# Start addresses of the moving operands, 64 bytes further from a multiple of 128, in a two-block transformer kernel

## The chip, the core and the metric

The kernel runs on one core of a Trainium2 chip. The metric is the time of one execution on the device in microseconds (us), the median of several runs.

## What is computed

Two transformer blocks follow each other on one sequence of 256 positions and width 2048, all in float32. Cut to the products with weights, which are nearly all of the work:

```python
# first block
h = rmsnorm(x, g_mix);   z = h @ w_in                  # 2048 -> 3584
kv = rmsnorm(mem, g_mem) @ w_kv                        # 2048 -> 1024, 256 memory rows
mix = concat(gated conv of z, pooled z @ pool_w, cross attention(q, k, v))
x = x + mix @ w_out                                    # 2048 -> 2048
u = causal_dwconv(rmsnorm(x, g_ffn) @ w_up) + bias     # 2048 -> 2 x 5632
x = rmsnorm(x + (silu(gate) * val) @ w_down, g_final)  # 5632 -> 2048
# second block
proj = rmsnorm(x, norm_attn_2) @ w_in_2                # 2048 -> 6144
x = x + concat(dilated attention, differential attention) @ w_out_2
h = rmsnorm(x, norm_ffn_2)
x = x + (silu(h @ w_gate_2) * (h @ w_up_2)) @ w_down_2
return rmsnorm(x, norm_final_2)
```

## The kernel before

**Split operands.** The products run in the type fp32r. To keep precision, every weight and every activation is split into a high part (its fp32r rounding) and a low part (the rest), and three of the four part products are added. An activation tile holds both parts side by side: 256 columns of high parts, then 256 of low parts, so 512 columns of 4 bytes.

**Blocks.** The weights come as blocks of 128 x 128. Each block makes two TensorE products into one accumulator of 512 columns: a *long* one (line 206: the block's high part, stationary, against all 512 columns, moving) and a *short* one (line 209: its low part against the 256 high columns). `products` takes blocks four at a time and orders them so that, in a steady stream of 16 blocks per output tile, TensorE does 8 longs, 8 shorts, 8 longs, and so on. Each product has its own load of 128 stationary columns (PEld), which the engine runs beside the product before it. So TensorE reads two streams from SBUF at a time: the moving columns of one product and the stationary columns of the next.

**Streams of weights.** A unit is 16 blocks, 1 MB. `prefetch` loads it three units ahead into a `raw` buffer by SyncE's queue, ScalarE copies it into a `hi` buffer (line 173), VectorE subtracts to get `lo` (line 185), half a unit at a time and two units ahead. The order of all engines is written out by hand, by a loop over quarters of a unit (`emit_all`); nothing in the change touches it.

**Moving tiles.** `A` holds the normalised activations that feed `w_in`, `w_up`, the q and k products of the second block, and `w_gate_2`/`w_up_2`: 3776 blocks. `M` holds the memory's (64 blocks). One buffer with the tag `mix` holds, one after another, `M`, `mix` (256 blocks of `w_out`), `hid` (1408 blocks of the two down products, in parts of 16, 14 and 14 rows of the hidden layer) and `y` (256 blocks of `w_out_2`). Six tiles `poolHL` feed 14 blocks. `hid` in the stages of 16 rows, `mix` and `A` meet the same order of instructions: 16 blocks per output tile.

**V products.** For the V projections the roles change (`vs_unit`, lines 273 to 275): 128 columns of `A` or `M` are stationary and 512 columns of `hi` or `lo` move: three products each, 384 products on `A` and 96 on `M`.

**Where tiles lie.** Every tile is a range of bytes in each partition, and the pools lie one behind the other. `raw`, `hi` and `lo` have sizes that are multiples of 128, so all of them start 32 bytes behind a multiple of 128. `X` and `A` follow and start at 32 too. Then comes the tag `stg` (first tile `mem`, 16448 bytes, which is 64 more than a multiple of 128), so the tag `mix` and all behind it start at 96. Columns are taken in steps of 512 bytes, so these remainders hold for every operand.

Of the kernel before, what the change touches and what calls it, by code (L numbers as in the profile page):

```python
# [10 lines left out]
F32 = mybir.dt.float32  # L11
F32R = mybir.dt.float32r
# [6 lines left out]
P = 128  # L19
D = 2048  # L20
S = 256
KT = D // P
# [77 lines left out]
def tile_two_blocks(ctx: ExitStack, tc: tile.TileContext, a: dict, out: bass.AP):  # L100
# [6 lines left out]
    big = pool("big", 1)  # L107
# [10 lines left out]
    vec = cst.tile([P, NCOL], F32, name="vec")  # L118
    ones = cst.tile([P, P], F32, name="ones")
    ident = kc[:, K_IDENT:K_IDENT + P]  # L120
    X = big.tile([P, KT, S], F32, name="X")
    A = big.tile([P, KT, 2 * S], F32R, name="A")

    def gain(name, kt):
        c = GAINS.index(name) * KT + kt
        return vec[:, c:c + 1]
# [61 lines left out]
    def weights(i, c0, c1):  # L188
        j = 2 * i + c0 // HB
        hi, lo = halves[j]  # L190
        c = slice(c0 % HB, (c1 - 1) % HB + 1)
        return hi[:, c], lo[:, c]
# [7 lines left out]
    def products(blocks):  # L200


        mm = nc.tensor.matmul

        def long(acc, hi, lo, x, first, last):
            mm(acc, lhsT=hi, rhs=x, start=first, stop=last)  # L206

        def short(acc, hi, lo, x, first, last):
            mm(acc[:, S:], lhsT=lo, rhs=x[:, :S], start=False, stop=False)  # L209

        opening = [b for b in blocks if b[4]]
        closing = [b for b in blocks if b[5]]
        between = [b for b in blocks if not b[4] and not b[5]]
        if longs[0] and not closing:
            for b in opening + between:
                long(*b)
            for b in blocks:
                short(*b)
            longs[0] = False
        else:  # L220
            for b in opening:
                long(*b)
            if opening and not closing:
                for b in between:
                    long(*b)
            for b in blocks:
                short(*b)
            if not opening or closing:
                for b in between:
                    long(*b)  # L230
            for b in closing:
                long(*b)
            longs[0] = bool(closing) or not opening
# [27 lines left out]
    def vs_unit(src, act, g, accs):  # L261

        def emit(i, b):
            if g == 0 and b == 0:
                for _ in range(2):
                    ac = acc_p.tile([P, 512], F32, tag="acc", name="acc")
                    accs.append(ac)
            kt = 4 * g + b
            x = act()[:, kt, :]
            hi, lo = weights(i, b * 512, (b + 1) * 512)  # L270
            for t in range(2):
                xh, xl = x[:, t * P:(t + 1) * P], x[:, S + t * P:S + (t + 1) * P]
                nc.tensor.matmul(accs[t], lhsT=xh, rhs=hi, start=kt == 0, stop=False)  # L273
                nc.tensor.matmul(accs[t], lhsT=xh, rhs=lo, start=False, stop=False)  # L274
                nc.tensor.matmul(accs[t], lhsT=xl, rhs=hi, start=False, stop=kt == KT - 1)  # L275

        return add_unit(src, UB * P, emit)
# [111 lines left out]
    def put_act(kt, g, x, a, norm):  # L389

        hi = a[:, kt, :S]
        nc.scalar.activation(hi, x, AF.Copy, scale=g)  # L392
        norm.add(x)
        yield
        nc.vector.scalar_tensor_tensor(out=a[:, kt, S:], in0=x, scalar=g, in1=hi.bitcast(F32),  # L395
                                       op0=ALU.mult, op1=ALU.subtract)
# [36 lines left out]
    def softmax(src, scale, normalise=True):  # L433

        mx = sm.tile([P, 2], F32, tag="mx", name="mx")
        nc.vector.tensor_reduce(out=mx, in_=src, op=ALU.max, axis=AX.X, negate=True)
        if scale != 1.0:
# [34 lines left out]
        return pt  # L472


    stg = big.tile([P, KT + KT * S], F32, tag="stg", name="mem")
    gm = stg[:, :KT]
    mem_t = stg[:, KT:].rearrange("p (k t) -> p k t", k=KT)
    M = big.tile([P, KT, 2 * S], F32R, tag="mix", name="M")
    lam_in = t2.tile([P, 4, 64], F32, tag="t2", name="lam_in")

    def load_mem(k0, k1):
# [32 lines left out]
    def x_load(q):  # L514
        nc.sync.dma_start(X[:, 4 * q:4 * q + 4, :], a["x"][:, 4 * q:4 * q + 4, :])

# [7 lines left out]
    def lambdas():  # L524
# [3 lines left out]
        sl = sm.tile([P, 2], F32, tag="lam_s", name="lam_s", bufs=1)  # L528
        nc.vector.tensor_reduce(out=sl, in_=pr, op=ALU.add, axis=AX.X)
        nc.scalar.activation(sl, sl, AF.Exp)  # L530
# [10 lines left out]
    def mem_act(kt):  # L541
        x, g, hi = mem_t[:, kt, :], gm[:, kt:kt + 1], M[:, kt, :S]
        nc.vector.tensor_scalar(out=hi, in0=x, scalar1=g, scalar2=None, op0=ALU.mult)
        nc.vector.scalar_tensor_tensor(out=M[:, kt, S:], in0=x, scalar=g, in1=hi.bitcast(F32),
                                       op0=ALU.mult, op1=ALU.subtract)
# [4 lines left out]
    def x_act(kt):  # L550
        return put_act(kt, gain("g_mix", kt), X[:, kt, :], A, n_x)

# [26 lines left out]
    for g in range(4):  # L579
        vs_unit(a["w_v"][g], lambda: M, g, v_accs)  # L580

        def emit(i, b, g=g):
            kt = 4 * g + b
            if kt == 0:
# [3 lines left out]
                for _ in range(2):  # L588
                    ac = s_p.tile([P, 2 * S], F32, tag="s", name="acc_s")
                    k_accs.append(ac)  # L590
            products([(k_accs[m], *weights(i, (4 * b + m) * P, (4 * b + m + 1) * P), M[:, kt, :],
                       kt == 0, kt == KT - 1) for m in range(4)])
# [15 lines left out]
    mix = {}  # L608
# [129 lines left out]
    def residual(gname, norm, scaled_to=None):  # L738
        def add(dst, m, acc):
            nc.vector.tensor_tensor(out=dst, in0=acc[:, :S], in1=X[:, m, :], op=ALU.add)  # L740
            nc.vector.tensor_tensor(out=dst, in0=acc[:, S:], in1=dst, op=ALU.add)  # L741

        def twice(m, acc):
            x = t1.tile([P, S], F32, tag="t", name="xr")
            add(x, m, acc)
            nc.vector.tensor_scalar(out=X[:, m, :], in0=x, scalar1=gain("g_final", m), scalar2=None, op0=ALU.mult)
            norm.inner.add(x)
# [381 lines left out]
```

## Time and profile before

| | us |
|---|---|
| median of 3 runs (2203.36 to 2205.53) | 2204.1 |
| the profiled execution | 2204.54 |
| its span in the trace | 2202.7 |
| TensorE busy with products | 2182.8 |
| VectorE busy | 1603.5 |
| ScalarE busy | 1143.2 |

The profiled execution is 0.4 us above the median, and its span leaves 1.8 us outside the trace. The page of the profile gives busy times, the granted clock of TensorE in 40 slices, the chain of work that ended last, and groups of equal instructions. The timeline gives instructions in order of time, equal neighbours merged into one row with their count; the start of one row less the start of the row before is the time that the earlier run took from the engine. The durations in a row overlap, since a product begins before the one ahead of it has ended, so all paces here are taken from starts.

### The profile page before, as it was taken

The page shows a single profiled execution, that of the slowest core. Times are in us where ns is not written, and L with a number is a line of the kernel's source. Part 1 is how long each engine was busy: PE and PEld are TensorE (multiplying, and loading weights), DVE is VectorE, ACT ScalarE, POOL GpSimd, SP SyncE. Part 2 cuts the span into 40 slices and gives each one's busy share as a digit, 9 for nine tenths or more (in the row PEclk, how much of TensorE's full clock was granted, in tenths as well). Part 3 has the DMA queues.
Part 4 walks back from the last instruction along what each step waited for, and adds up shares of the span by engine and source line. Part 5 has one row for each costly group of instructions (what it writes and reads, how often), then busy time and mean ns, then how long its engine had stood idle before and what let it go on. Part 6 is the DMA issues. An engine that isn't in the chain of part 4 may idle for free.

```text
span 2202.7 us, 31334 instructions
## 1 busy us (share of the span) xinstructions
PE 2182.8 (99%) x12426; PEld 1909.5 (87%) x12426; DVE 1603.5 (73%) x2553; ACT 1143.2 (52%) x1738; POOL 106.7 (5%) x114
## 2 busy tenths in 40 slices
PE   8999999999999999999999999999999999999997
PEld 7888888888888888888888888888888888888886
DVE  8877778886588757878779677786665666666666
ACT  6555556564465536565456655464443444344442
POOL 4000010000000000003100000010000000000012
PEclk9999999999999999999999999999999999999998
DMA  7545555555555555555544444555555555555553
GB/s 285 197 169 177 191 188 193 189 192 191 191 191 186 190 182 192 188 192 188 194 167 158 161 165 153 179 203 186 185 186 192 191 189 191 191 192 186 185 184 115
DMA packets 60195, 408.99 MB, mean 186 GB/s; under 512 B 6672, under 2 KB 8592, under 8 KB 11792
## 3 DMA queue, kind: packets, MB, share of 16 engines
q1 hardware_dynamic: 60048, 406.99, 53.9%
q8 instruction: 97, 1.59, 0.3%
q14 instruction: 50, 0.41, 0.0%
HBM read 404.86 MB, written 2.10 MB: 185 GB/s over the span
## 4 chain that ended last, share of the span: by engine, by line
PE 97%; DVE 1%; DMA 1%; issue 0%; SPq 0%; ACT 0%; DVEq 0%; ACTq 0%
PE acc L206 60%; PE acc L209 31%; PE acc L273 1%; PE acc L274 1%; PE acc L275 1%; PE s_ps L430 1%; DVE lo L185 0%; DMA X<-in_x 0%; PE pT_ps L466 0%; PE o_ps L920 0%; PE o_ps L878 0%; DMA raw<-in_w_k 0%; DVE end L998 0%; PE nps L342 0%; PE o_ps L638 0%
## 5 line engine op out<-in xcount | busy, mean ns | idle before, releaser
L173 ACT ACTIVATE hi<-raw 128x1024 fp32r<-128x1024 f32 x758 | 799.2, 1057 | 583.2 <-PE acc L206 413.9
L185 DVE TENSOR_TENSOR lo<-raw,hi 128x1024 fp32r<-128x1024 f32 x758 | 933.5, 1239 | 145.4 <-ACT hi L173 133.4
L206 PE MATMUL acc<-A,hi 128*128 128x512 f32 x3776 | 961.6, 394 | 0.0
L206 PEld LDWEIGHTS acc<-A,hi 128*128 128x128 f32 x3776 | 677.3, 189 | 119.8 <-issue 1.0
L209 PEld LDWEIGHTS acc<-A,lo 128*128 128x128 f32 x3776 | 518.5, 190 | 39.2 <-issue 0.7
L209 PE MATMUL acc<-A,lo 128*128 128x256 f32 x3776 | 535.0, 283 | 0.0
L206 PE MATMUL acc<-hid,hi 128*128 128x512 f32 x1408 | 360.2, 392 | 0.0
L206 PEld LDWEIGHTS acc<-hid,hi 128*128 128x128 f32 x1408 | 250.6, 188 | 41.5
L414 ACT ACTIVATE z<-acc 128x256 f32<-128x256 f32 x244 | 91.8, 382 | 274.2 <-PE acc L206 274.1
L209 PEld LDWEIGHTS acc<-hid,lo 128*128 128x128 f32 x1408 | 195.3, 188 | 17.2
L209 PE MATMUL acc<-hid,lo 128*128 128x256 f32 x1408 | 199.6, 279 | 0.0
L740 DVE TENSOR_TENSOR X<-acc,X 128x256 f32<-128x256 f32 x128 | 54.0, 422 | 177.4 <-PE acc L206 177.3
L416 DVE TENSOR_TENSOR z<-acc,z 128x256 f32<-128x256 f32 x244 | 103.0, 422 | 103.4 <-ACT z L414 102.6
L715 DVE SCALAR_TENSOR_TENSOR c<-z,vec,c 128x255 f32<-128x255 f32 (+1 forms) x188 | 90.0, 480 | 5.1 <-ACT c L710 1.2
L404 DVE TENSOR_TENSOR hid<-hid 128x256 fp32r<-128x256 f32 x88 | 37.4, 425 | 77.1 <-ACT hid L402 77.1
L422 DVE TENSOR_TENSOR z<-z,R_ffn 128x256 f32<-128x256 f32 x176 | 74.7, 424 | 6.0
L206 PE MATMUL acc<-y,hi 128*128 128x512 f32 x256 | 65.4, 394 | 0.0
L206 PE MATMUL acc<-mix,hi 128*128 128x512 f32 x256 | 64.2, 392 | 0.0
L317 POOL TENSOR_TENSOR sq_attn<-sq_attn,sqt 128x256 f32<-128x256 f32 x30 | 29.4, 993 | 707.9 <-ACT sqt L315 707.7
L392 ACT ACTIVATE A<-X,vec 128x256 fp32r<-128x256 f32 x64 | 32.4, 507 | 57.8 <-DVE X L741 57.3
L741 DVE TENSOR_TENSOR X<-acc,X 128x256 f32<-128x256 f32 x128 | 54.3, 424 | 4.4
L395 DVE SCALAR_TENSOR_TENSOR A<-X,vec,A 128x256 fp32r<-128x256 f32 x64 | 50.6, 802 | 8.3 <-ACT A L392 8.3
(174 smaller groups left out, 1347.5 us busy)
## 6 DMA issues: line engine op xcount, KB each, us to landing
raw<-in_w_up SPq DMA_DIRECT2D x88, 1024.0 KB, 4.9
raw<-in_w_down SPq DMA_DIRECT2D x88, 1024.0 KB, 4.9
raw<-in_w_gu SPq DMA_DIRECT2D x88, 1024.0 KB, 4.9
raw<-in_w_out SPq DMA_DIRECT2D x32, 1024.0 KB, 4.9
raw<-in_w_in SPq DMA_DIRECT2D x22, 1024.0 KB, 4.9
raw<-in_w_qkb SPq DMA_DIRECT2D x16, 1024.0 KB, 4.8
raw<-in_w_qka SPq DMA_DIRECT2D x16, 1024.0 KB, 4.9
raw<-in_w_vb SPq DMA_DIRECT2D x8, 1024.0 KB, 4.8
```

The source lines that it names most:

```text
L173: nc.scalar.activation(hi[:, :n], raws[i][:, c0:c0 + n], AF.Copy)
L185: nc.vector.tensor_tensor(out=lo[:, :n], in0=raws[i][:, c0:c0 + n], in1=hi[:, :n].bitcast(F32), op=ALU.subtract)
L206: mm(acc, lhsT=hi, rhs=x, start=first, stop=last)
L209: mm(acc[:, S:], lhsT=lo, rhs=x[:, :S], start=False, stop=False)
L395: nc.vector.scalar_tensor_tensor(out=a[:, kt, S:], in0=x, scalar=g, in1=hi.bitcast(F32), op0=ALU.mult, op1=ALU.subtract)
L404: nc.vector.tensor_tensor(out=hl[:, S:], in0=src, in1=h.bitcast(F32), op=ALU.subtract)
L414: nc.scalar.activation(z, acc[:, S:], AF.Copy)
L416: nc.vector.tensor_tensor(out=z, in0=acc[:, :S], in1=z, op=ALU.add)
L422: nc.vector.tensor_tensor(out=d, in0=z, in1=R, op=ALU.mult)
L715: nc.vector.scalar_tensor_tensor(out=c[:, s:], in0=z[:, :S - s], scalar=w[2 - s], in1=c[:, s:], op0=ALU.mult, op1=ALU.add)
L740: nc.vector.tensor_tensor(out=dst, in0=acc[:, :S], in1=X[:, m, :], op=ALU.add)
L741: nc.vector.tensor_tensor(out=dst, in0=acc[:, S:], in1=dst, op=ALU.add)
```

## The change

Two tile requests are added or moved; no instruction is. A tile `home` of 64 bytes, which nothing writes or reads, is put ahead of `X` and `A`, and the tag `mix` is asked for ahead of `stg`. On every engine the same instructions stand in the same order as before.

```diff
     ident = kc[:, K_IDENT:K_IDENT + P]
+
+    big.tile([P, 16], F32, name="home")
     X = big.tile([P, KT, S], F32, name="X")
     A = big.tile([P, KT, 2 * S], F32R, name="A")
...
+    M = big.tile([P, KT, 2 * S], F32R, tag="mix", name="M")
     stg = big.tile([P, KT + KT * S], F32, tag="stg", name="mem")
     gm = stg[:, :KT]
     mem_t = stg[:, KT:].rearrange("p (k t) -> p k t", k=KT)
-    M = big.tile([P, KT, 2 * S], F32R, tag="mix", name="M")
```

What that does to the start addresses, as the built programs have them (bytes; in brackets the remainder by 128):

| tile | before | after |
|---|---|---|
| `hi`, `lo` (first buffers) | 50720 (32), 67104 (32) | the same |
| `X` | 83488 (32) | 83552 (96) |
| `A` | 99872 (32) | 99936 (96) |
| `M`, `mix`, `hid`, `y` | 149088 (96) | 132704 (96) |
| `mem`, `kqv`, `vv`, `end` | 132640 (32) | 165472 (96) |
| sums of squares, `t1`, `t2`, `qk`, `poolHL` | (96) | (32) |

So relative to `hi` and `lo`, `A` goes from a distance of 0 to one of 64, `mix`, `hid`, `y` and `M` stay at 64, and the small `poolHL` goes from 64 to 0.

## Rows read from the trace of the kernel before

**Rows 1.** Page: TensorE busy, granted clock in 40 slices, chain by engine
```profile
PE 2182.8 (99%) x12426; PEld 1909.5 (87%) x12426; DVE 1603.5 (73%) x2553; ACT 1143.2 (52%) x1738; POOL 106.7 (5%) x114
PEclk9999999999999999999999999999999999999998
PE 97%; DVE 1%; DMA 1%; issue 0%; SPq 0%; ACT 0%; DVEq 0%; ACTq 0%
```
**Rows 2.** Waits of PE, longest first: us in total, times, longest
```profile
PE acc L274 <- DVE lo L185: 3.1, 2, 2.6
```
**Rows 3.** Page, groups of products on A and hid: busy us, mean ns
```profile
L206 PE MATMUL acc<-A,hi 128*128 128x512 f32 x3776 | 961.6, 394 | 0.0
L206 PE MATMUL acc<-hid,hi 128*128 128x512 f32 x1408 | 360.2, 392 | 0.0
...
L273 PE MATMUL acc<-hi,A 128*128 128x512 f32 x128 | 51.2, 400 | 0.0
```
**Rows 4.** Timeline of PE, up stage on A: start, us, what, count
```profile
341.07 2.00 PE L206 MATMUL acc<-A,hi 128*128 128x512 f32 x8
342.91 1.11 PE L209 MATMUL acc<-A,lo 128*128 128x256 f32 x8
343.86 2.00 PE L206 MATMUL acc<-A,hi 128*128 128x512 f32 x8
...
486.32 2.00 PE L206 MATMUL acc<-A,hi 128*128 128x512 f32 x8
```
**Rows 5.** Timeline of PE, output product of the first block, on mix
```profile
240.63 2.00 PE L206 MATMUL acc<-mix,hi 128*128 128x512 f32 x8
...
309.58 2.00 PE L206 MATMUL acc<-mix,hi 128*128 128x512 f32 x8
```
**Rows 6.** Timeline of PE, first down stage (16 rows), on hid
```profile
508.59 2.00 PE L206 MATMUL acc<-hid,hi 128*128 128x512 f32 x8
510.43 1.11 PE L209 MATMUL acc<-hid,lo 128*128 128x256 f32 x8
511.38 2.00 PE L206 MATMUL acc<-hid,hi 128*128 128x512 f32 x8
513.21 1.07 PE L209 MATMUL acc<-hid,lo 128*128 128x256 f32 x8
514.12 1.99 PE L206 MATMUL acc<-hid,hi 128*128 128x512 f32 x8
...
577.54 2.00 PE L206 MATMUL acc<-hid,hi 128*128 128x512 f32 x8
```
**Rows 7.** Timeline of PE, second down stage (14 rows), one round of 28 blocks
```profile
761.57 2.00 PE L206 MATMUL acc<-hid,hi 128*128 128x512 f32 x8
...
771.27 2.00 PE L206 MATMUL acc<-hid,hi 128*128 128x512 f32 x8
```
**Rows 8.** Timeline of PE, K product of the memory: 16 blocks on M
```profile
23.50 0.63 PE L206 MATMUL acc<-M,hi 128*128 128x512 f32 x2
...
25.37 0.63 PE L206 MATMUL acc<-M,hi 128*128 128x512 f32 x2
...
27.22 0.40 PE L209 MATMUL acc<-M,lo 128*128 128x256 f32 x2
...
29.08 0.40 PE L273 MATMUL acc<-hi,M 128*128 128x512 f32 x1
```
**Rows 9.** Timeline of PE, V products, 20 apart, on M and on A
```profile
18.60 0.39 PE L273 MATMUL acc<-hi,M 128*128 128x512 f32 x1
...
23.26 0.40 PE L275 MATMUL acc<-hi,M 128*128 128x512 f32 x1
...
1063.09 0.39 PE L273 MATMUL acc<-hi,A 128*128 128x512 f32 x1
...
1067.63 0.39 PE L275 MATMUL acc<-hi,A 128*128 128x512 f32 x1
```
**Rows 10.** Windows: stretch, length, busy of PE, PEld, DVE, ACT, POOL; clock; DMA
```profile
340.00:490.00 150.00, 150.00 (x862) 132.12 (x861) 124.11 (x193) 91.31 (x137) 0.00 (x0) 1.00 0.55 190
```

## The prediction

> **What bounds the kernel now.** I read the page first. TensorE has a product in flight for 2182.8 of 2202.7 us, at its upper clock level (2.4 GHz) in nearly every slice, and the chain of work that ended last runs through it for 97% of the span [rows 1]. The waits come next: TensorE waits for seven causes in all, and the largest of them comes to 3.1 us [rows 2]. So neither weights, DMA nor evictions hold it; its own pace per product sets the time, and a change helps or hurts by the nanoseconds that it moves in that pace, times a large count.
>
> A busy share of 99% hides that pace, because products overlap: a mean of 394 ns per long product on `A` against 392 on `hid` [rows 3] looks like nothing. So I went to the timeline and took starts from starts. In the first up stage, on `A`, a run of 8 longs takes 342.91 - 341.07 = 1.84 us and a run of 8 shorts 343.86 - 342.91 = 0.95 us. From the first row there to the last, 145.25 us, lie 52 such rounds of 8 blocks, so 2.793 us a round or **349.2 ns a block** [rows 4]. The stage on `mix` has 25 rounds in 309.58 - 240.63 = 68.95 us: 2.758 us a round or **344.75 ns a block** [rows 5]. The first stage on `hid` has 25 rounds in 577.54 - 508.59 = 68.95 us, the same number [rows 6]. There the longs take 1.83 or 1.84 us, and the shorts alternate between 0.95 us (510.43 to 511.38) and 0.91 us (513.21 to 514.12).
>
> This is the reading that matters. TensorE's instructions are the same in these stages: 16 blocks per output tile, in the same runs. What differs for TensorE is the tile that moves, and it differs in where it starts: `A` at a distance of 0 from the weight parts, modulo 128, `mix` and `hid` at 64. The kernel of before already holds both layouts, and the one at 64 is faster by 349.2 - 344.75 = 4.4 ns a block, or 1.3%.
>
> Other explanations fit worse. It is not the load on the other engines: VectorE is busy 124.11 of 150 us in the up stage [rows 10], and evictions come once in 16 blocks, so contention with them would slow a round here and there; instead, every round has the same length. It is not the clock, granted at 1.00 in that stretch [rows 10] as in the stages compared.
>
> **The change part by part.** It adds and removes no instruction, no wait and no transfer, and moves none past a queue. What changes is which address each operand has.
>
> *Blocks on A, distance 0 to 64.* There are 3776 of them [rows 3], all in outputs of 16 blocks each, the form of the stages on `mix` and `hid`. All of them lie on the path. At the price of those two stages: 3776 x 4.4 ns = **-16.6 us**. For the bounds I take the other rows at distance 64. The second down stage has 14 blocks per output and so shorter runs: one round of 28 blocks takes 771.27 - 761.57 = 9.70 us, 346.4 ns a block [rows 7]; at that price the gain is 3776 x 2.8 = 10.6 us. The 16 blocks of the K product on `M` take 29.08 - 23.50 = 5.58 us, 348.75 ns a block [rows 8], only 0.4 ns below `A`: 1.5 us in all. I take 4.4 ns, because the two stages that give it have the same run lengths as those on `A`; the blocks on `M` begin afresh after every 24 V products, at the start of the kernel. The row on `M` is the far end of this term, and it counts in the chance of no change. The q and k products and part of the `w_in` products are broken by attention work; a little of the 4.4 may be lost there, which the bound of 2.8 covers.
>
> *V products on A, distance 0 to 64.* Here the change costs. Twenty steps on `A` take 1067.63 - 1063.09 = 4.54 us, 227 ns each; twenty on `M`, whose tile already lies at 64, take 23.26 - 18.60 = 4.66 us, 233 ns each [rows 9]. With 3 x 128 = 384 products on `A` [rows 3]: 384 x 6 ns = **+2.3 us**. The lower bound is 0, if the slower pace on `M` belongs to the kernel's start; nothing speaks for a gain.
>
> *Blocks on poolHL, 64 to 0.* 14 blocks x 4.4 ns = +0.06 us.
>
> *Blocks on mix, hid, y and M.* They keep their distance: 0.
>
> *Other operands.* The attention products and transposes read `vv`, `probs`, `pT` and `qk`; between two such tiles that shift alike nothing changes, and the few where the distance does change are short. VectorE, ScalarE and the DMAs read and write the same amounts at shifted addresses. I take 0 for all of it. For bounds: no row shows one of their instructions at both addresses, and a change of some per cent either way would fall under TensorE's stream, since VectorE has 150 - 124.11 = 26 us free in 150 of a busy stage [rows 10]. If that cover were gone, TensorE would begin to wait for `lo`, as it does now only at the start [rows 2].
>
> *Does a faster TensorE meet another bound?* It would take 1.3% less per unit in the stages on `A`. VectorE's share there would go from 83% to 84%, and the DMA engines' from 0.55 to 0.56 [rows 10]. Neither binds, so no gain is given back.
>
> **The sum.** -16.6 + 2.3 + 0.06 = -14.2 us. The profiled execution took 2204.54 us, so 2190.3; it lies 0.4 us above the median, and against the median of 2204.1 this gives 2189.9. I say **2190 us**, 0.64% faster. With the lower price per block it is 2204.1 - 10.6 + 2.3 = 2196; with the higher price and free V products 2204.1 - 16.6 = 2187.5.
>
> **The rivals.** *The offset is not the cause.* Then `A` is slower than `mix` and `hid` for a reason that the change leaves alone, say who reads the accumulators in those stages (ScalarE and VectorE on `A`, VectorE alone on `hid`), and the blocks keep 349.2 ns. The time stays at 2204, or 2206 with the dearer V products. For it speaks the price on `M`, which lies at 64 and hardly gains [rows 8]. Against it speaks that every round on `A` is slow, not the ones beside an eviction, and that `mix` and `hid`, 200 us apart and with different neighbours, agree to the last digit [rows 5, 6]. The Trainium skill has a rule on this side: its page "TensorE: Matmul & The Clock Gate", Part 2, step 1, says that TensorE reads the moving operand and the weights through two independent SBUF ports, so that loading the next weights takes no bandwidth from the running product. By that rule no distance between the two streams would matter, and this rival would hold; the two paces on equal instructions speak against it here, without proving that the address makes them.
>
> *The offset slows long products.* In the V products, which are long ones without a break, the tile at 64 is the slower one, 233 against 227 ns [rows 9]. If that were the true effect of the distance, and the short products owed their pace on `mix` and `hid` to something else, the longs on `A` would go from 1.84 us / 8 = 230 ns to 233: 3776 x 3 = 11.3 us, and with the V products 2204.1 + 11.3 + 2.3 = 2218 us. It decides against the change from the point where 8 longs lose more than the 0.03 us that 8 shorts gain on average. Against it: at 64, the longs on `hid` take 1.83 to 1.84 us [rows 6], and those on `M` 27.22 - 25.37 = 1.85 us [rows 8], so in blocks the longs hardly change.
>
> *The change doesn't do what it says.* The addresses of the built programs say that it does; I give this nothing of its own.
>
> **How the numbers follow.** I give the forecast a chance of 0.84, with 2187 to 2197 as its own range, the first rival 0.10 and the second 0.06. The range that holds 8 times in 10 is the forecast's with 1 us at each end for the terms set to zero: 2186 to 2198. What can be told from no change in this kernel is about 0.2%, 4.4 us; the whole of the forecast lies beyond that, so the chances are 0.84 for faster, 0.10 for the same, 0.06 for slower.
>
> **What would show it.** In the profile after, rounds of 8 blocks on `A` in the up and gate stages should start 2.76 us apart instead of 2.79, with shorts that alternate between 0.95 and 0.91 us a run, as on `hid` now; the stages on `mix` and `hid` should keep theirs. The V products on `A` in the second block should step by 233 ns instead of 227. TensorE's waits should stay near 10 us. The prediction is wrong if rounds on `A` still start 2.79 us apart (first rival), if its longs grow past 1.87 us a run (second), or if the rounds on `hid` move although their distance didn't.

## The result, and the profile after

The changed kernel takes **2191.8 us** (median of 4 runs, 2190.65 to 2192.53) against 2203.8 us of the kernel before in the same comparison: a ratio of 0.9943, with a 95% interval from 0.9931 to 0.9956. That is 0.57% faster, 9.7 to 15.2 us by the interval. The profiled execution took 2190.65 us against 2204.54, and its span fell from 2202.7 to 2188.8 us, 13.9 us.

The head of the page after, to be read beside [rows 1]: TensorE is as full as before, only for less long.

```profile
PE 2169.9 (99%) x12426; PEld 1896.8 (87%) x12426; DVE 1600.6 (73%) x2553; ACT 1143.9 (52%) x1738; POOL 108.2 (5%) x114
```

The groups of products on `A`, `hid` and the V products on `A`, with the shapes kept apart (busy us, mean ns; lines are 2 higher than before):

```profile
L208 PE MATMUL acc<-A,hi 128*128 128x512 f32 x3776 | 957.2, 393 | 0.0
L211 PE MATMUL acc<-A,lo 128*128 128x256 f32 x3776 | 523.4, 279 | 0.0
...
L208 PE MATMUL acc<-hid,hi 128*128 128x512 f32 x1408 | 360.1, 392 | 0.0
L211 PE MATMUL acc<-hid,lo 128*128 128x256 f32 x1408 | 199.7, 279 | 0.0
...
L275 PE MATMUL acc<-hi,A 128*128 128x512 f32 x128 | 51.8, 405 | 0.0
L276 PE MATMUL acc<-lo,A 128*128 128x512 f32 x128 | 50.6, 396 | 0.0
L277 PE MATMUL acc<-hi,A 128*128 128x512 f32 x128 | 50.6, 395 | 0.0
```

Of the kernel before, the groups that go with those in [rows 3]:

```profile
L209 PE MATMUL acc<-A,lo 128*128 128x256 f32 x3776 | 535.0, 283 | 0.0
...
L275 PE MATMUL acc<-hi,A 128*128 128x512 f32 x128 | 50.0, 391 | 0.0
L274 PE MATMUL acc<-lo,A 128*128 128x512 f32 x128 | 49.9, 390 | 0.0
```

With [rows 3], the blocks on `A` were busy 961.6 + 535.0 = 1496.6 us and are now 1480.6: 16.0 us less, 11.6 of them in the short products. The V products on `A` went from 151.1 to 153.0 us, 1.9 us more. Products on `hid` stay within 0.1 us. 16.0 - 1.9 = 14.1 us, near the 13.9 that the span lost. (A run of longs and the run of shorts behind it overlap in these busy times; the split by starts stands under "The terms".)

The timeline of TensorE in the up stage shows the pace itself, to be read beside [rows 4] and [rows 6] (start, us, what, count):

```profile
338.87 1.99 PE L208 MATMUL acc<-A,hi 128*128 128x512 f32 x8
340.70 1.11 PE L211 MATMUL acc<-A,lo 128*128 128x256 f32 x8
341.64 2.00 PE L208 MATMUL acc<-A,hi 128*128 128x512 f32 x8
343.47 1.07 PE L211 MATMUL acc<-A,lo 128*128 128x256 f32 x8
344.38 1.99 PE L208 MATMUL acc<-A,hi 128*128 128x512 f32 x8
...
482.21 1.99 PE L208 MATMUL acc<-A,hi 128*128 128x512 f32 x8
```

Shorts on `A` now alternate between 341.64 - 340.70 = 0.94 us and 344.38 - 343.47 = 0.91 us a run of 8, as on `hid` in [rows 6]; before, every run took 0.95. From first row to last lie 52 rounds of 8 blocks: 143.34 us / 416 = 344.6 ns a block, where it was 349.2.

The V products on `A` after (timeline, 20 steps apart) went the other way, as those on `M` in [rows 9]: 4.66 us / 20 = 233 ns, where it was 227.

```profile
1055.07 0.39 PE L275 MATMUL acc<-hi,A 128*128 128x512 f32 x1
...
1059.73 0.39 PE L277 MATMUL acc<-hi,A 128*128 128x512 f32 x1
```

TensorE's waits after have the same size as [rows 2]; nothing else became late:

```profile
PE acc L211 <- DVE lo L187: 2.3, 1, 2.3
```

### The profile page after: what moved, and what is told of

Its sections match the earlier page's. It is cut to its first block, busy times and chain, and to the rows that moved or that the text cites. A ratio compares the mean times of both kernels' runs of the same rounds, so it can differ in the third digit from the quotient of the medians.

```text
span 2188.8 us, 31334 instructions
## 1 busy us (share of the span) xinstructions
PE 2169.9 (99%) x12426; PEld 1896.8 (87%) x12426; DVE 1600.6 (73%) x2553; ACT 1143.9 (52%) x1738; POOL 108.2 (5%) x114
## 4 chain that ended last, share of the span: by engine, by line
PE 97%; DVE 1%; DMA 1%; issue 0%; ACT 0%; DVEq 0%; SPq 0%; ACTq 0%
PE acc L208 60%; PE acc L211 30%; PE acc L275 1%; PE acc L276 1%; PE acc L277 1%; PE s_ps L432 1%; DMA raw<-in_w_k 1%; DVE lo L187 0%; PE pT_ps L468 0%; PE o_ps L922 0%; PE o_ps L880 0%; DVE M L545 0%; DVE end L1000 0%; DVE M L546 0%; PE nps L344 0%; DMA mem<-in_mem 0%
## 5 line engine op out<-in xcount | busy, mean ns | idle before, releaser
L208 PE MATMUL acc<-A,hi 128*128 128x512 f32 x3776 | 957.2, 393 | 0.0
L211 PEld LDWEIGHTS acc<-A,lo 128*128 128x128 f32 x3776 | 509.3, 188 | 40.9 <-issue 0.7
L211 PE MATMUL acc<-A,lo 128*128 128x256 f32 x3776 | 523.4, 279 | 0.0
```

## The experiments

In all twelve kernels only addresses differ. "Distance" is the start of the activation tile (`A`, `M`, `mix`, `hid`, `y`) less that of the weight part. In blocks the activation tile moves. In V products it stands and the weights move, so there the start of the moving operand less that of the stationary one is minus this distance.

**Is it the distance, or where the moving tile lies?** 64 unused bytes ahead of all weight buffers move everything behind them by 64, so all distances stay as before.

```diff
+    cst.tile([P, 16], F32, name="shift")
     X = big.tile([P, KT, S], F32, name="X")
```

> The kernel before with 64 unused bytes ahead of raw, hi and lo, so that all of these and all behind them move by 64: hi and lo at 96, A at 96, mix and hid at 32 (remainders by 128). Every distance stays as before. If the distance between moving columns and weight parts sets the pace: A 349.2 ns a block, mix and hid 344.75, V products on A 227 ns, time 2204 us. If instead the remainder of the moving tile itself does (96 fast, 32 slow): A 344.75 (-16.6 us), the 1920 blocks on mix, hid and y 349.2 (+8.4 us), so about 2196 us.

Measured: 2204.2 us, ratio 0.9999 (0.999 to 1.0009). Timeline, up stage on `A` and first down stage on `hid`:

```profile
340.49 2.00 PE L207 MATMUL acc<-A,hi 128*128 128x512 f32 x8
...
485.74 2.00 PE L207 MATMUL acc<-A,hi 128*128 128x512 f32 x8
...
508.01 2.00 PE L207 MATMUL acc<-hid,hi 128*128 128x512 f32 x8
...
576.96 2.00 PE L207 MATMUL acc<-hid,hi 128*128 128x512 f32 x8
```

52 rounds on `A` at 349.2 ns a block, 25 on `hid` at 344.75: the paces of before to the digit, though `A` now starts at a remainder of 96 and `hid` at 32. To move all of them by 64 together does nothing.

**One part of the change alone.** The exchange of `M` and `mem` without `home` brings `mix`, `hid`, `y` and `M` to a distance of 0 too.

```diff
-    big.tile([P, 16], F32, name="home")
```

> The changed kernel without the tile home: only the exchange of M and mem. All moving tiles lie at a distance of 0. If the distance sets the pace: A stays at 349.2 ns a block, and 1984 blocks on mix, hid, y and M go from 344.75 to 349.2: +8.8 us, V products on M gain 96 x 6 ns = 0.6 us: 2212 us. If the stages on mix and hid are faster for another reason than the address: 2204 us.

Measured: 2211.1 us, ratio 1.0032 (1.002 to 1.0044). Timeline, first down stage on `hid`:

```profile
512.30 2.00 PE L207 MATMUL acc<-hid,hi 128*128 128x512 f32 x8
...
579.33 2.00 PE L207 MATMUL acc<-hid,hi 128*128 128x512 f32 x8
```

24 rounds in 67.03 us: 349.1 ns a block on a tile that had 344.75. So the stages on `hid` owe their pace to the address, not to who reads their accumulators, and the first rival falls. It also shows that the half of the change without the other half would have cost 7 us.

**Other distances.** The tile `home` of the changed kernel gets 8, 24, 32, 40, 48, 56 or 64 columns in place of 16, so that all moving tiles of the blocks but the small `poolHL` lie at 32, 96, 128, 160, 192, 224 or 256.

```diff
-    big.tile([P, 16], F32, name="home")
+    big.tile([P, 8], F32, name="home")
```

> The changed kernel with a home tile of 32 bytes instead of 64: all moving tiles at a distance of 32. No row shows this distance. If only the coincidence at 0 is slow, as at 64: 345 ns a block on A and hid, 2192 us. If 64 is the one good distance and 32 lies half way: 347 ns, about 2202 us. If 32 counts as 0: 349.2 ns, 2212 us.

> The changed kernel with a home tile of 128 bytes: all moving tiles at a distance of 128. If the pattern repeats every 128 bytes, this is a distance of 0: 349.2 ns a block everywhere, V products 227 ns, 2212 us. If it repeats at 256 or later: another pace, and with the pace of 64 about 2192 us.

> All moving tiles at a distance of 256. Distances of 0 and 128 gave different paces (349.2 and 351.2 ns a block on A; V products 228 and 232 ns), so the pattern doesn't repeat at 128. If it repeats at 256: as at 0, 349.2 ns, V products on A 228 ns, about 2211 us. If at 512 or later: another pace, in blocks or V products.

> All moving tiles at a distance of 192, which is 64 short of 256. If the sign of the distance doesn't matter and the pattern repeats at 256: as at 64, 345.0 ns a block on A and 233 ns for V products, 2192 us. If it does matter, or repeats later: another pace.

> All moving tiles at a distance of 96, between 64 (345.0 ns a block) and 128 (351.2 ns). If pace changes evenly with the distance: 348 ns a block, about 2206 us. If 64 is a good distance by itself and odd multiples of 32 are dear, as 32 is: 350 ns, 2218 us.

> All moving tiles at a distance of 160. If the odd multiples of 32 are dear, as 32 (350.1 ns a block on A) and 96 (353.3 ns) are: 350 to 353 ns, 2216 to 2237 us. If the second half of 256 is the cheaper one, as 192 (346.9 ns) against 128 (351.2 ns) hints: 347 to 349 ns, 2200 to 2211 us.

> All moving tiles at a distance of 224, the last multiple of 32 under 256. If odd multiples of 32 are dear: 350 to 353 ns a block, 2216 to 2237 us. If the pace changes evenly from 192 (346.9 ns) to 256 (349.2 ns): 348 ns, 2205 us.

First and last run of longs in the up stage on `A`, timeline of each kernel. At 32 (50 rounds between the rows):

```profile
342.27 2.03 PE L208 MATMUL acc<-A,hi 128*128 128x512 f32 x8
...
482.27 2.03 PE L208 MATMUL acc<-A,hi 128*128 128x512 f32 x8
```

At 96 (50 rounds):

```profile
339.63 2.03 PE L208 MATMUL acc<-A,hi 128*128 128x512 f32 x8
...
480.96 2.03 PE L208 MATMUL acc<-A,hi 128*128 128x512 f32 x8
```

At 128 (50 rounds):

```profile
341.12 2.02 PE L208 MATMUL acc<-A,hi 128*128 128x512 f32 x8
...
481.62 2.02 PE L208 MATMUL acc<-A,hi 128*128 128x512 f32 x8
```

At 160 (50 rounds):

```profile
341.14 2.03 PE L208 MATMUL acc<-A,hi 128*128 128x512 f32 x8
...
481.92 2.04 PE L208 MATMUL acc<-A,hi 128*128 128x512 f32 x8
```

At 192 (51 rounds):

```profile
340.90 2.02 PE L208 MATMUL acc<-A,hi 128*128 128x512 f32 x8
...
482.35 2.02 PE L208 MATMUL acc<-A,hi 128*128 128x512 f32 x8
```

At 224 (50 rounds):

```profile
341.41 2.02 PE L208 MATMUL acc<-A,hi 128*128 128x512 f32 x8
...
482.07 2.02 PE L208 MATMUL acc<-A,hi 128*128 128x512 f32 x8
```

At 256 (50 rounds):

```profile
341.16 2.00 PE L208 MATMUL acc<-A,hi 128*128 128x512 f32 x8
...
480.83 2.00 PE L208 MATMUL acc<-A,hi 128*128 128x512 f32 x8
```

The table gives the block from those rows, and beside it the mean steps from start to start of longs, shorts and V products on `A` over the whole trace (steps over 300 ns, or over 160 ns for shorts, left out; they are about 1% of the blocks' steps and 4% of the V products'):

| distance | ns a block | long, short | V product | time, us | ratio to before (95%) |
|---|---|---|---|---|---|
| 0 (all) | 349.2 | 230.4, 118.9 | 228 | 2211.1 | 1.0032 (1.002 to 1.0044) |
| 32 | 350.0 | 233.3, 116.7 | 233 | 2218.0 | 1.0064 (1.0049 to 1.0079) |
| 64 (the change) | 344.6 | 229.2, 115.9 | 233 | 2191.8 | 0.9943 (0.9931 to 0.9956) |
| 96 | 353.3 | 233.2, 120.1 | 234 | 2236.6 | 1.0146 (1.0117 to 1.0175) |
| 128 | 351.3 | 232.7, 118.5 | 232 | 2223.0 | 1.0086 (1.0069 to 1.0103) |
| 160 | 352.0 | 233.8, 117.9 | 233 | 2227.2 | 1.0105 (1.0086 to 1.0123) |
| 192 | 346.7 | 232.7, 114.2 | 229 | 2200.4 | 0.9982 (0.997 to 0.9993) |
| 224 | 351.7 | 232.7, 118.9 | 233 | 2226.6 | 1.0102 (1.0083 to 1.012) |
| 256 | 349.2 | 230.4, 118.9 | 228 | 2211.5 | 1.0031 (1.0018 to 1.0045) |

256 is 0 over again, in blocks and in V products, and 128 is not: among these steps the pattern repeats at 256. It is not even and not symmetric: 32 and 224, 96 and 160, 64 and 192 differ. 64 has the best blocks of the eight, 0 the best V products. At 32 all three expectations missed: 2218.0 us lies above the dearest of them. The expectation of a period of 128 missed as well, and so did those that the sign doesn't matter (192), that the pace changes evenly (96, 224) and that the second half is cheaper (160). That odd multiples of 32 are dear was then expected three times and held each time, though 96, at 2236.6 us, is far dearer than the 2218 said.

The V products fit the longs once the sign is minded. A row of 64 in the table puts their moving operand at -64, which is 192 modulo 256, and the row of 192 puts it at 64. There they are quick (timeline at 192, 20 steps: 4.58 us, 229 ns):

```profile
1052.65 0.39 PE L275 MATMUL acc<-hi,A 128*128 128x512 f32 x1
...
1057.23 0.39 PE L277 MATMUL acc<-hi,A 128*128 128x512 f32 x1
```

By the start of the moving operand less that of the stationary one, modulo 256, longs in blocks take 230.4 ns at 0, 229.2 at 64 and 232.7 to 233.8 at the other six steps; V products take 228 at 0, 229 at 64 and 232 to 234 at the other six. So both kinds of 512 columns are quick at 0 and 64. The shorts have another order, with 192 (114.2) the best and 64 (115.9) next.

**Can long and short products be set apart?** `hi` was moved by 64 bytes, `lo` by 128 and the moving tiles by 192, since each pad shifts all that lies behind it. Modulo 128 that leaves `lo` where it was.

```diff
+    whi_p.tile([P, 16], F32, tag="pad", name="pad_hi", bufs=1)
+    wlo_p.tile([P, 16], F32, tag="pad", name="pad_lo", bufs=1)
     big.tile([P, 16], F32, name="home")
```

> hi moved to 96 and lo left at 32, moving tiles at 96: a distance of 0 to hi and 64 to lo (a multiple of 128 aside). If the distance to the part that is loaded beside the running product sets the pace of each kind apart: longs as at 0 (230.4 ns, or 227 once a run of longs has settled), shorts as at 64 (115.9 ns), 343 to 346 ns a block, 2186 to 2196 us. If the two kinds can't be taken apart: 349 ns, 2211 us.

Measured: 2211.9 us, ratio 1.0033 (1.0019 to 1.0047). The expectation took a multiple of 128 for nothing. By remainders of 256 the moving tiles lay at 128 from `hi` and 64 from `lo`, so this was not the trial that it was meant to be. Read with the right distances it is one all the same. Groups of the page:

```profile
L210 PE MATMUL acc<-A,hi 128*128 128x512 f32 x3776 | 968.5, 396 | 0.0
...
L213 PE MATMUL acc<-A,lo 128*128 128x256 f32 x3776 | 526.2, 279 | 0.0
```

The page of the kernel with all at 128 has 970.3 and 533.7 us in these groups, that with all at 64 has 957.2 and 523.4. So the longs take nearly what 128 gives and the shorts nearly what 64 gives.

The trial was made again with `hi` at the distance that is best for longs in the table, 64, and `lo` at the best for shorts, 192:

```diff
-    big.tile([P, 16], F32, name="home")
+    wlo_p.tile([P, 32], F32, tag="pad", name="pad_lo", bufs=1)
+    big.tile([P, 48], F32, name="home")
```

> lo moved so that the moving tiles lie at 64 from hi and at 192 from lo (remainders by 256). If longs follow the distance to hi and shorts that to lo: 229.1 + 114.2 = 343.3 ns a block, 1.7 ns less on 5760 blocks, 2182 us. If each kind also feels the other part, whose load runs beside it where the kinds meet: between 345 and 347 ns, 2192 to 2200 us.

Measured: 2186.65 us, ratio 0.9921 (0.9907 to 0.9934). Up stage on `A`, 51 rounds, and one round of 28 blocks of the second down stage:

```profile
341.80 2.00 PE L209 MATMUL acc<-A,hi 128*128 128x512 f32 x8
...
481.88 2.00 PE L209 MATMUL acc<-A,hi 128*128 128x512 f32 x8
...
754.26 2.00 PE L209 MATMUL acc<-hid,hi 128*128 128x512 f32 x8
...
763.98 2.00 PE L209 MATMUL acc<-hid,hi 128*128 128x512 f32 x8
```

343.3 ns a block in unbroken runs. The 343.3 that was expected came from means over the whole trace, and by that measure the blocks on `A` take 229.7 + 114.4 = 344.1 ns: longs near what 64 gives (229.2), shorts near what 192 gives (114.2). So the two kinds can be set apart. The V products agree. In the same stretch, on `A`, those whose moving part is `lo`, at 64 by moving less stationary, step by 229.1 ns in the mean, and those whose moving part is `hi`, at 192, by 232.5. This speaks against a rival that the runs before it leave open, that the moving columns meet the writes of ScalarE and VectorE into `hi` and `lo`: those run beside products of every kind, while each kind follows the distance to its own weight part.

The whole kernel gains 5.1 us over the change by the medians, 3.8 by the spans, and not 10: in unbroken runs the change stood at 344.6 already, so the step is 1.3 ns and not 1.7, and where runs are short it is lost (the second down stage takes 9.72 us for 28 blocks against 9.70 in [rows 7]).

**Is the V term the distance too?** In the changed kernel the `hi` and `lo` halves of the V units are put 64 bytes further on in longer buffers, so that V products lie at 0 and blocks stay at 64.

```diff
+    def half(pool, tag, j):
+        o = 16 if j // 2 in V_UNITS else 0
+        return pool.tile([P, HB + 64], F32R, tag=tag, name=f"{tag}{j}")[:, o:o + HB]
...
-        hi = whi_p.tile([P, HB], F32R, tag="hi", name=f"hi{j}")
+        hi = half(whi_p, "hi", j)
...
-        lo = wlo_p.tile([P, HB], F32R, tag="lo", name=f"lo{j}")
+        lo = half(wlo_p, "lo", j)
...
```

> The changed kernel, but the hi and lo halves of the V units lie 64 bytes further on in buffers made 256 bytes longer, so the V products on A and M have a distance of 0 and the blocks keep 64. If the V term is a matter of the distance alone: V products on A from 233 to 228 ns (384 x 5.2 = 2.0 us), on M likewise (0.5 us), blocks unchanged at 345.0 ns: 2189 us. If the slower V products came from the place of A and not from its distance: 2192 us, 233 ns.

Measured: 2188.8 us, ratio 0.9932 (0.9918 to 0.9945). Timeline, V products on `A`, 14 steps apart:

```profile
1054.67 0.39 PE L280 MATMUL acc<-hi,A 128*128 128x512 f32 x1
...
1057.84 0.39 PE L282 MATMUL acc<-hi,A 128*128 128x512 f32 x1
```

3.17 us / 14 = 226 ns, the old pace, while the groups of blocks on `A` keep 957.2 and 523.4 us. The span fell from 2188.8 to 2186.6, by 2.2 us of the 2.5 expected.

The runs of both last versions (2186.45 to 2187.08 us and 2188.39 to 2189.73) lie below those of the change. The intervals of their ratios overlap with the change's, so the order of the three rests on these runs and on the spans (2185.0, 2186.6, 2188.8). The two together were not run.

## Why the prediction was right

**The reading that carried it.** The prediction took the price of the new layout from stages of the old kernel that already had it, on equal instructions. That held to 0.2 ns: `A` at 64 runs at 344.6 ns a block, `mix` and `hid` ran at 344.75 [rows 5, 6]. The experiments that move all tiles together, and that bring `hid` to 0, show that the address makes this pace.

**The terms.** Blocks on `A`: -16.6 us forecast, -16.0 by the groups. By the starts of the stages it is -15.4: the up and gate stages gave 12.5 us on 2816 blocks, 4.4 ns each as priced, and the other 960 blocks, of `w_in`, q and k, gave 2.9 us, 3.0 ns each. These are the stages that other products break, as the text feared, and the bound of 2.8 ns was near the mark for them. V products: +2.3 forecast, +1.9 by the groups and +2.0 by starts, and the step of 233 ns was right. 15.4 - 2.0 = 13.4 us; the other 0.5 of the span is an earlier start of the first products with weights (5.0 us against 5.5; it lies between 4.8 and 5.5 in the kernels here), which belongs to no term. `mix`, `hid`, waits and the other engines: 0, as forecast. `poolHL`: +0.06 forecast, and there the sign was wrong: its longs went from 234.1 to 231.0 ns a step and its shorts from 118.1 to 117.3, 0.05 us in all for 14 blocks. By remainders of 256 they went from a distance of 64 to 128, not to 0. They come in runs of two or three between blocks on `A`, whose distance changed at the same time; why they gained was not tried. The sum of -14.2 stands against -13.9 in the span; the forecast for the profiled execution, 2190.3 us, against 2190.65. The median, 2191.8, is 1.8 above the 2190 said: by medians the gain is 12.0 us, and the 14.2 lies inside its interval of 9.7 to 15.2.

**Two steps that failed without harm.** All distances were counted modulo 128. The pattern repeats at 256, and 128 differs from 0. The prediction was safe only because `mix` and `hid` before and `A` after lie at 64 modulo 256 as well; with a `home` of 192 bytes the same argument modulo 128 would have promised 2190 us, and the chip gave 2200.4. The other step is the sign in the V products. The prediction put them at 64, like the blocks, where their moving operand lies at 192. Their price held because `M` before and `A` after have the same layout in them.

**The rivals.** The first fell with the kernel that has every distance at 0. Its evidence stays true: of the stretches of 16 blocks on `M` that no wait breaks, three take 5.53 to 5.59 us before, at 64, and two take 5.58 in that kernel, at 0. In these short runs the two distances cost nearly the same. The second rested on that sign: the V products that it took for slow longs at 64 are longs at 192, and there the longs in blocks are slow too (232.7 ns). At 64 they take 229.2, against 230.4 at 0. What is left of the rival is that 0 suits a stream without shorts. In full runs of 8 longs on `A` before, the mean steps by place in the run are 233, 235, 229, 232, 231, 227, 227 and 227 ns; after, they lie between 227.6 and 230.3 at every place. So at 0 the longs soon after shorts are the dear ones, and settled ones keep the 227 of the V products. The last experiment uses that.

The rule cited with the first rival, from the Trainium skill's page "TensorE: Matmul & The Clock Gate" (Part 2, step 1), says that loading the next weights takes no SBUF bandwidth from the running product. What the prediction drew from it, that no distance would matter, doesn't hold in these runs: with nothing but addresses changed, a block takes between 344.6 and 353.3 ns. Whether it is bandwidth that is lost, no run shows.

**What stays open.** Why these distances are the good ones, why the first longs of a run are dear at 0, and which part of the chip the two streams share, no run here tells. Distances between the multiples of 32 were not tried.

## What to carry to other kernels

When TensorE hardly waits, compare its pace on equal instructions between stages with different operands, from start to start, before looking for work to remove. The distance between the addresses of the moving and the stationary operand can be worth 2% of the whole. Count it from moving to stationary, also where the roles of weights and activations change. Here, modulo 256, 64 and then 192 were best for runs of 8 longs and 8 shorts, 0 for unbroken long products with 64 close behind, and others cost up to 1.5% of the kernel's time. Any edit that resizes a buffer ahead of such tiles shifts that distance, so a small slowdown after an unrelated edit may be nothing else.

## What the runs showed that was not expected

The size of the swing: from 2186.65 us to 2236.6, 2.3%, by padding alone. Also its form: a period of 256 bytes, with no symmetry around 0 for the blocks, and a distance of 32 that is worse for the blocks (350.0 ns) than full coincidence (349.2), while 64, 32 bytes on, is the best of all (344.6).
